# Partition sums of the later modulation vectors: 32 columns of ones in four column groups, then one product that turns rows into columns

## The chip, the cores and the metric

One core of one Trainium2 chip. The time is the device time of one execution in microseconds (us), and a kernel is given by the median of its runs. PE is TensorE (matrix products), DVE is VectorE, ACT is ScalarE, POOL is GpSimd, and SP issues the DMAs. SBUF is the memory on the core that the engines read, with 128 partitions; PSUM is the memory that PE writes its products into.

## The reference, cut to what matters

The block is one layer of a hybrid backbone: a combined input projection feeds four GLA heads and four mLSTM heads, an output projection follows, and then a SwiGLU MLP with a 3x3 depthwise convolution. Each sub-layer is modulated by vectors computed from the condition `c`:

```python
c_act = jax.nn.silu(c)
mod = (c_act @ w_mod + b_mod)[:, None, :]
sh1, sc1, gt1, sh2, sc2, gt2 = jnp.split(mod, 6, axis=-1)
...
x = x + gt1 * merge_groups(...)
h2 = rmsnorm(x, g_norm2) * (1 + sc2) + sh2
x = x + gt2 * conv_ffn(h2, ...)
```

`c` is one vector of 2048 numbers, `w_mod` is 2048 x 12288, all in float32. The model width is 2048, there are 512 latent tokens and 256 context tokens, and the MLP is 5504 wide. The change is in how `gt1`, `sh2`, `sc2` and `gt2` are summed, which the kernel calls regions 2, 3, 4 and 5.

## The kernel before, in words

Every large product is made of three products of rounded halves (`mm3`: high x high, high x low, low x high), so each 512 KB block of weights is loaded, cast to a high half on ACT (L89) and to the remaining low half on DVE (L90), and then used by 24 or 36 products on PE. `load_split` does this. The loaded block lives in the pool `wraw`, which has four buffers; the high and low halves have two buffers each. The projections of the eight heads come first (`project_steps`, eight blocks for each head, tiles `a`), with the recurrent stages of the head before woven into them by `weave`; then the gates (`unit`, tiles `ga`), the output projection (`wo`), and the MLP, where `up_gate` and `up_val` alternate (tiles `ug` and `uv`, eight blocks of weights each, the number behind them is the group of four feature tiles) and `down_block` follows (`dn`). While the products of `uv` run, DVE makes the convolution of the group before, tile `cv`, with eight instructions for each of four tiles.

The modulation vectors of regions 2 to 5 are made beside all this. Each region has four groups of 512 outputs. For each group, `mod_chunk` loads eight 512 KB blocks of `w_mod` into the same four `wraw` buffers. In each block the even half is multiplied by its part of `c_act` and summed on DVE (L252, L255, tile `sum0`), the odd half is scaled on ACT (L253, L256) and summed on POOL (L257, tile `sum1`). After the eighth, POOL adds the two sums (L259). What is left is a tile of 128 partitions x 512 columns whose sum over the partitions is wanted, as four columns of 128. `mod_end` makes it with four PE products, each with 128 x 128 of the tile as the stationary operand and one column of ones as the moving one, and DVE adds the bias.

These steps are "fillers": a list of small functions that `load_split` works off, so many for each block of weights:

```python
credit[0] += rate[0]
while credit[0] >= 1:
    credit[0] -= 1
    if fillers:
        fillers.pop(0)()
```

`rate` is 2 for blocks 3 to 7 of an mLSTM head (and 0 for blocks 0 to 2), and 1.5 in the gates, the output projection and the MLP, so there one block of weights takes one filler and the next two. `mod_fillers` lists the eight chunks of a group, `lag - 1` empty fillers, and `mod_end`. With `lag` 3 a group takes 11 fillers in regions 2 to 4. In region 5 it takes 10, behind 20 empty ones.

The products of heads and fillers are kept in program order on PE (`pinned` and `keep_in_program_order`); the order of the other engines is made by a scheduler, which also decides which buffer of a pool a tile gets. Small PSUM results, among them `mc` of `mod_end`, `pg` and `po` of the mLSTM heads, and the new `mr`, share the pool `psB`, which has two buffers.

Of the kernel before, what the change touches and what calls it, by code (L numbers as in the profile page):

```python
# [11 lines left out]
F32 = mybir.dt.float32  # L12
# [6 lines left out]
P = 128  # L19
# [25 lines left out]
C_ONE = C_SA + 32  # L45
# [24 lines left out]
def block_kernel(ctx: ExitStack, tc: tile.TileContext, a: dict, out: bass.AP):  # L70
    nc = tc.nc
    V, S, G, PE = nc.vector, nc.scalar, nc.gpsimd, nc.tensor

    def pool(stack, name, bufs=1, space=None, waits="pool"):
        if space is None:
            return stack.enter_context(tc.tile_pool(name=name, bufs=bufs, reuse_waits=waits))
        return stack.enter_context(tc.tile_pool(name=name, bufs=bufs, space=space))
# [7 lines left out]
    def add(o, x, y):  # L85
        V.tensor_tensor(out=o, in0=x, in1=y, op=ALU.add)
# [23 lines left out]
    keep = pool(ctx, "keep")  # L110
    cst = keep.tile([P, C_END], F32, name="cst")
# [12 lines left out]
    def cc(off, n=P, p=P):  # L124
        return cst[0:p, off : off + n]

    ident = cc(C_ID)
    ones = cst[:, C_ONE : C_ONE + 1].to_broadcast([P, P])
# [6 lines left out]
    def psb(name, shape=(P, T)):  # L135
        return psB.tile(list(shape), F32, name=name, tag="psb")
# [20 lines left out]
    fillers = []  # L157
# [84 lines left out]
    def mod_chunk(region, n, kp, parts):  # L242

        name = f"m{region}_{n}_{kp}"
        raw = wraw.tile([P, 2, T], F32, name=f"raw_{name}", tag="raw")
        nc.sync.dma_start(raw, a["w_mod2"][region - 2, n, kp])
        if kp == 0:
            parts += [sum_tile(i, name) for i in range(2)]
        dv, po = parts
        ce, co = (csil[:, 2 * kp + i : 2 * kp + i + 1] for i in range(2))  # L250
        if kp == 0:
            V.tensor_scalar(out=dv, in0=raw[:, 0, :], scalar1=ce, scalar2=None, op0=ALU.mult)  # L252
            S.activation(po, raw[:, 1, :], AF.Copy, scale=co)  # L253
        else:
            V.scalar_tensor_tensor(out=dv, in0=raw[:, 0, :], scalar=ce, in1=dv, op0=ALU.mult, op1=ALU.add)  # L255
            S.activation(raw[:, 1, :], raw[:, 1, :], AF.Copy, scale=co)  # L256
            G.tensor_tensor(out=po, in0=po, in1=raw[:, 1, :], op=ALU.add)  # L257
        if kp == KP - 1:
            G.tensor_tensor(out=po, in0=po, in1=dv, op=ALU.add)  # L259

    def mod_end(region, n, parts):

        po = parts[1]
        ps = psb(f"mc{region}_{n}", (P, 4))
        for i in range(4):
            tc.keep_in_program_order(PE.matmul(ps[:, i : i + 1], po[:, P * i : P * i + P], cst[:, C_ONE : C_ONE + 1],
                                               start=True, stop=True))
        o = modc[region][:, 4 * n : 4 * n + 4]
        add(o, ps, bmod[:, 16 * region + 4 * n : 16 * region + 4 * n + 4])
        if region == 4:  # L270
            V.scalar_tensor_tensor(out=o, in0=o, scalar=1.0, in1=gn2[:, 4 * n : 4 * n + 4], op0=ALU.add, op1=ALU.mult)

    def mod_fillers(regions, lag):

        for region in regions:
            for n in range(4):
                parts = []
                for kp in range(KP):
                    fillers.append(lambda r=region, n=n, kp=kp, p=parts: mod_chunk(r, n, kp, p))
                fillers.extend([lambda: None] * (lag - 1))  # L280
                fillers.append(lambda r=region, n=n, p=parts: mod_end(r, n, p))

    def sum_tile(i, name):
# [218 lines left out]
    for c0, n, hs, m in ((0, T, hx, gm[0]), (T, TC, hc, gm[1])):  # L502
        ps = psb(f"gm{c0}", (P, n))
        for k in range(KT):
            g = 32 * (k % 4)
            parts = [h[k].bitcast(F32) for h in hs]
            if hs is hx and not 4 <= k < 8:
                parts = [xl[k]]
            for i, part in enumerate(parts):
                mm(ps[g : g + 32, :], wsm[:, k, :], part, start=(k < 4 and i == 0),  # L510
                   stop=(k >= 12 and i == len(parts) - 1), skip_group_check=True)
# [360 lines left out]

    yT = []
    mod_fillers((2, 3, 4), 3)
    pinned[0] = True
    preps = [{} for _ in range(H)]
# [142 lines left out]
        return fp.tile([P, T], F32, name=f"sum{i}_{name}", tag=f"g{'hl'[i]}10")  # L1019

    rate[0] = 1.5
    fillers += [lambda: None] * 20
    mod_fillers((5,), 2)

    def up_gate(q):
        accs = unit(a["w_up4"][2 * q] if q < 10 else a["w_up3"][0], f"ug{q}", *h2, n=QUADS[q])
# [152 lines left out]
def build(nc, arrays):  # L1179
    ins = {k: nc.dram_tensor(f"in_{k}", v.shape, mybir.dt.from_np(v.dtype), kind="ExternalInput").ap()  # L1180
           for k, v in arrays.items()}
    out = nc.dram_tensor("out_0", (KT, P, T), F32, kind="ExternalOutput").ap()
    with tile.TileContext(nc) as tc:
        block_kernel(tc, ins, out)
# [8 lines left out]
```

## Time and profile before

| what | value |
|---|---|
| median of three runs | 2600.23 us (2597.21 to 2606.91) |
| the profiled execution, its own time | 2597.59 us |
| span of that profile | 2595.9 us |
| busy share of PE, DVE, ACT, POOL | 98%, 52%, 34%, 9% |
| granted clock of TensorE, mean | 0.994 |

The span is the time from the first to the last instruction in the profile; 1.7 us of the execution lie around it. A row of the timeline gives the start in us from the start of the span, the length, the engine, the line, the operation, and the tiles (output, an arrow, inputs), with the shape of the weights as partitions*columns and of the moving operand. A number with an arrow in brackets is the idle time of the engine before the row and what ended it. Products on PE overlap, so their rhythm is read from start to start, not from their lengths. Float32 products appear as two rows each, so the 64 products of `mod_end` are 128 rows. `PEld` is the loading of weights.

### The profile page before, as it was taken

How to read it: one execution, taken by the hardware profiler on the slowest of the kernel's cores; microseconds unless marked ns; L12 is line 12 of the kernel's file. 1: busy time of each engine (PE TensorE's matmuls, PEld its weight loads, DVE VectorE, ACT ScalarE, POOL GpSimd, SP SyncE). 2: the span in 40 equal slices, each digit the busy share in tenths (PEclk: the TensorE clock that was granted, in tenths of full speed). 3: DMA queues.
4: the chain of work that ended last, by engine and by line, in shares of the span. 5: the costliest groups of instructions: out<-in, count | busy, mean ns of one | idle time of the engine just before them, and what ended most of it. 6: DMA issues, size and time to landing. Idle time of an engine off the chain costs nothing.

```text
span 2595.9 us, 31962 instructions
## 1 busy us (share of the span) xinstructions
PE 2541.1 (98%) x12882; PEld 2134.8 (82%) x12882; DVE 1356.0 (52%) x1969; ACT 873.9 (34%) x1289; POOL 228.1 (9%) x183
## 2 busy tenths in 40 slices
PE   6999999999999999999999999999999999999998
PEld 4887888888897888878878888888888888888887
DVE  6557765543334465458576336532653365336544
ACT  4225543332333343334433123312331233123332
POOL 0000001021222323210321000000000000000001
PEclk9999999999999999989999999999999999999999
DMA  9741112121333666532654222322232223222333
GB/s 383 269 155 34 33 41 90 66 98 66 122 122 126 214 226 216 199 114 101 211 178 141 96 97 97 98 97 98 98 98 98 97 98 97 96 96 87 100 97 102
DMA packets 96349, 321.39 MB, mean 124 GB/s; under 512 B 10884, under 2 KB 15304, under 8 KB 96200
## 3 DMA queue, kind: packets, MB, share of 16 engines
q1 hardware_dynamic: 96200, 319.34, 35.8%
q8 instruction: 101, 1.65, 0.3%
q14 instruction: 48, 0.39, 0.0%
HBM read 315.10 MB, written 4.19 MB: 123 GB/s over the span
## 4 chain that ended last, share of the span: by engine, by line
PE 89%; DVE 4%; DMA 4%; issue 1%; ACT 1%; POOL 1%; SPq 0%; POOLq 0%; ACTq 0%; DVEq 0%
PE a L95 18%; PE ug L95 18%; PE dn L95 17%; PE uv L95 17%; PE wo L95 6%; PE ga L95 5%; PE po L95 3%; DMA raw_m<-in_w_mod 2%; PE sl L95 1%; PE ps_m L95 1%; DVE cv L1040 1%; PE dl L95 1%; PE cst L95 0%; POOL sum_m L257 0%; PE s L95 0%
## 5 line engine op out<-in xcount | busy, mean ns | idle before, releaser
L95 PE MATMUL ug<-h2h,hi_ug 128*128 128x512 f32 x688 | 269.0, 392 | 1.6 <-ACT h2h L999 1.6
L95 PE MATMUL uv<-h2h,hi_uv 128*128 128x512 f32 x688 | 268.6, 390 | 1.5 <-ACT hi_uv L89 1.5
L95 PE MATMUL uv<-h2h,lo_uv 128*128 128x512 f32 x688 | 268.5, 390 | 1.4 <-DVE lo_uv L90 1.4
L95 PE MATMUL ug<-h2l,hi_ug 128*128 128x512 f32 x688 | 268.4, 390 | 0.0
L95 PE MATMUL ug<-h2h,lo_ug 128*128 128x512 f32 x688 | 268.4, 390 | 0.0
L95 PE MATMUL uv<-h2l,hi_uv 128*128 128x512 f32 x688 | 268.4, 390 | 0.0
L95 PE MATMUL dn<-gh,hi_d 128*128 128x512 f32 x644 | 250.5, 389 | 0.0
L95 PE MATMUL dn<-gl,hi_d 128*128 128x512 f32 x644 | 250.5, 389 | 0.0
L95 PE MATMUL dn<-gh,lo_d 128*128 128x512 f32 x644 | 250.5, 389 | 0.0
L1040 DVE SCALAR_TENSOR_TENSOR cv<-pad,cwt,cv 128x512 f32<-128x512 f32 x344 | 242.8, 765 | 10.6 <-ACT cv L1038 9.1
L90 DVE TENSOR_TENSOR lo_ug<-raw_ug,hi_ug 128x1024 fp32r<-128x1024 f32 (+1 forms) x88 | 107.3, 1220 | 240.0 <-ACT hi_ug L89 240.0
L257 POOL TENSOR_TENSOR sum_m<-sum_m,raw_m 128x512 f32<-128x512 f32 x112 | 175.6, 1568 | 576.2 <-ACT raw_m L256 335.7
L90 DVE TENSOR_TENSOR lo_uv<-raw_uv,hi_uv 128x1024 fp32r<-128x1024 f32 (+1 forms) x88 | 105.6, 1200 | 181.1 <-ACT hi_uv L89 180.6
L90 DVE TENSOR_TENSOR lo_d<-raw_d,hi_d 128x1024 fp32r<-128x1024 f32 x82 | 98.8, 1205 | 165.5 <-ACT hi_d L89 164.6
L89 ACT CAST hi_ug<-raw_ug 128x1024 fp32r<-128x1024 f32 (+1 forms) x88 | 90.9, 1033 | 266.6 <-PE ug L95 199.2
L89 ACT CAST hi_d<-raw_d 128x1024 fp32r<-128x1024 f32 x82 | 85.1, 1037 | 278.7 <-PE dn L95 224.4
L255 DVE SCALAR_TENSOR_TENSOR sum_m<-raw_m,csil,sum_m 128x512 f32<-128x512 f32 x112 | 97.9, 874 | 150.6 <-DMA raw_m<-in_w_mod 150.4
L89 ACT CAST hi_uv<-raw_uv 128x1024 fp32r<-128x1024 f32 (+1 forms) x88 | 90.9, 1033 | 251.0 <-PE uv L95 180.9
L95 PEld LDWEIGHTS uv<-h2h,lo_uv 128*128 128x128 f32 x688 | 129.6, 188 | 29.6 <-DVE lo_uv L90 2.7
L95 PEld LDWEIGHTS ug<-h2h,hi_ug 128*128 128x128 f32 x688 | 129.9, 189 | 28.9 <-ACT h2h L999 1.9
L95 PEld LDWEIGHTS uv<-h2h,hi_uv 128*128 128x128 f32 x688 | 129.4, 188 | 28.9 <-ACT hi_uv L89 2.0
L95 PEld LDWEIGHTS ug<-h2l,hi_ug 128*128 128x128 f32 x688 | 129.7, 189 | 27.0
(304 smaller groups left out, 5220.4 us busy)
## 6 DMA issues: line engine op xcount, KB each, us to landing
raw_m<-in_w_mod SPq DMA_DIRECT2D x192, 512.0 KB, 4.4
raw_ug<-in_w_up SPq DMA_DIRECT2D x80, 512.0 KB, 3.2
raw_uv<-in_w_up SPq DMA_DIRECT2D x80, 512.0 KB, 3.2
raw_d<-in_w_down SPq DMA_DIRECT2D x79, 512.0 KB, 3.3
raw_h<-in_w_heads SPq DMA_DIRECT2D x64, 512.0 KB, 3.2
raw_ga<-in_w_gates SPq DMA_DIRECT2D x32, 512.0 KB, 3.4
raw_wo<-in_w_out SPq DMA_DIRECT2D x32, 512.0 KB, 4.3
xl<-in_xT SPq DMA_DIRECT2D x16, 256.0 KB, 4.8
```

The costliest lines, as they stand in the source:

```text
L89: S.copy(hi, x)
L90: return V.tensor_tensor(out=lo, in0=x, in1=hi.bitcast(F32), op=ALU.subtract).ins
L95: ins = PE.matmul(*args, **kw)
L255: V.scalar_tensor_tensor(out=dv, in0=raw[:, 0, :], scalar=ce, in1=dv, op0=ALU.mult, op1=ALU.add)
L257: G.tensor_tensor(out=po, in0=po, in1=raw[:, 1, :], op=ALU.add)
L1040: V.scalar_tensor_tensor(out=t3, in0=src, scalar=w, in1=t3, op0=ALU.mult, op1=ALU.add)
```

## The change

`mod_end` is split. The new `mod_sums` makes four products with the roles exchanged: 32 columns of ones are the stationary operand, 128 columns of the sum tile the moving one, and the results go to the partitions 0 to 31, 32 to 63, 64 to 95 and 96 to 127 of one PSUM tile `mr`. Each of them is a row of 128 sums, repeated 32 times. ACT copies the 128 x 128 tile to SBUF (`mrow`, one buffer). `mod_end` then makes one product with `mrow` as the stationary operand and columns 0, 32, 64 and 96 of the identity as the moving one, which yields the four columns. The DVE addition stays.

In `mod_fillers` the last empty filler becomes `mod_sums`, so `mod_sums` stands one filler ahead of `mod_end`. Regions 2 to 4 keep 11 fillers for a group. Region 5 goes from 20 empty fillers and 10 for each group to 16 empty ones and 11 for each group; both make 60.

```diff
+    def mod_sums(region, n, parts):
+
+        po = parts[1]
+        ps = psb(f"mr{region}_{n}", (P, P))
+        for i in range(4):
+            tc.keep_in_program_order(PE.matmul(ps[32 * i : 32 * i + 32, :], ones[:, 0:32], po[:, P * i : P * i + P],
+                                               start=True, stop=True, skip_group_check=True))
+        parts.append(keep.tile([P, P], F32, name=f"mrow{region}_{n}", tag="mrow"))
+        with tc.high_priority():
+            S.copy(parts[2], ps)
+
     def mod_end(region, n, parts):
 
-        po = parts[1]
         ps = psb(f"mc{region}_{n}", (P, 4))
-        for i in range(4):
-            tc.keep_in_program_order(PE.matmul(ps[:, i : i + 1], po[:, P * i : P * i + P], cst[:, C_ONE : C_ONE + 1],
-                                               start=True, stop=True))
+        tc.keep_in_program_order(PE.matmul(ps, parts[2], ident[:, 0 : P : 32], start=True, stop=True))
         o = modc[region][:, 4 * n : 4 * n + 4]
         add(o, ps, bmod[:, 16 * region + 4 * n : 16 * region + 4 * n + 4])
...
-                fillers.extend([lambda: None] * (lag - 1))
+                fillers.extend([lambda: None] * (lag - 2))
+                fillers.append(lambda r=region, n=n, p=parts: mod_sums(r, n, p))
                 fillers.append(lambda r=region, n=n, p=parts: mod_end(r, n, p))
...
-    fillers += [lambda: None] * 20
-    mod_fillers((5,), 2)
+    fillers += [lambda: None] * 16
+    mod_fillers((5,), 3)
```

Where `mod_sums` and `mod_end` fall relative to each other depends on the fillers that one block of weights takes. In ten of the sixteen groups they belong to different blocks, with 24 or more rows of PE between them. In five, all at rate 1.5 (groups 0 and 3 of region 3, group 2 of region 4, groups 0 and 3 of region 5), they belong to one block and four products stand between them. In one, group 1 of region 2, nothing stands between them.

Three places show it. The first is PE in the last mLSTM head (head 7), where `pg70` and `pg71` are the two products that feed the exponentials of that head through `psB`. Before:

```order
L95 MATMUL pg70_6622<-negg_95,cst_58 128x512
L95 MATMUL pg71_6635<-negg_95,cst_58 128x512
L95 MATMUL ga0_0_6576<-hTh2_554,hi_ga0_1_6649 128x512
L95 MATMUL ga0_0_6576<-hTl2_555,hi_ga0_1_6649 128x512
L95 MATMUL ga0_0_6576<-hTh2_554,lo_ga0_1_6650 128x512
```

and now:

```order
L95 MATMUL pg70_6634<-negg_95,cst_58 128x512
L95 MATMUL pg71_6647<-negg_95,cst_58 128x512
L266 MATMUL mr2_3_6666<-sum1_m2_3_0_6331,cst_58 32x128 x4
L95 MATMUL ga0_0_6588<-hTh2_554,hi_ga0_1_6661 128x512
L95 MATMUL ga0_0_6588<-hTl2_555,hi_ga0_1_6661 128x512
L95 MATMUL ga0_0_6588<-hTh2_554,lo_ga0_1_6662 128x512
```

The sums of group 3 of region 2 (`mr2_3`) now stand directly behind the two products that fill both buffers of `psB`; the old `mc2_3` stood 24 rows further on, behind the products `cst70` and `cst71`, where it still stands in its new form.

The second place is group 1 of region 2, on PE and on ACT, at the end of block 2 of head 6 (tiles `a6`). Now, on PE:

```order
L95 MATMUL a6_5_5255<-lo_h6_2_5423,hch5_748 128x384
L95 MATMUL a6_5_5255<-hi_h6_2_5422,hcl5_749 128x384
L266 MATMUL mr2_1_5564<-sum1_m2_1_0_4905,cst_58 32x128 x4
L275 MATMUL mc2_1_5571<-cst_58,mrow2_1_5569 128x4
L95 MATMUL a6_0_5250<-hTh6_939,hi_h6_3_5559 128x512
```

and on ACT, where `mrow2_1` is the copy that the second of these products needs:

```order
L146 ACTIVATE scr5_5611<-var5_5610 128x4
L147 ACTIVATE rs5_5612<-scr5_5611 128x4
L89 CAST hi_h6_4_5651<-raw_h6_4_5650 128x1024
L270 COPY mrow2_1_5569<-mr2_1_5564 128x128
L253 ACTIVATE sum1_m2_2_0_5659<-raw_m2_2_0_5656,csil_61 128x512
```

Before, one row `mc2_1` of four products stood in the place of the two on PE, and the sum of the next group followed the cast on ACT directly; the copy has moved in between, behind the cast.

The third place is SP, which issues the loads, in `up_val` of group 1 (`raw_uv1`, blocks of weights) with the chunks of group 2 of region 5 (`raw_m5_2`). Before:

```order
L164 DMA raw_uv1_3_10512<-in_w_up4 128x1024
L246 DMA raw_m5_2_0_10518<-in_w_mod2 128x1024
L246 DMA raw_m5_2_1_10524<-in_w_mod2 128x1024
L164 DMA raw_uv1_4_10553<-in_w_up4 128x1024
L246 DMA raw_m5_2_2_10559<-in_w_mod2 128x1024
L164 DMA raw_uv1_5_10588<-in_w_up4 128x1024
L246 DMA raw_m5_2_3_10594<-in_w_mod2 128x1024
L246 DMA raw_m5_2_4_10599<-in_w_mod2 128x1024
L164 DMA raw_uv1_6_10628<-in_w_up4 128x1024
```

and now:

```order
L164 DMA raw_uv1_3_10579<-in_w_up4 128x1024
L246 DMA raw_m5_2_2_10585<-in_w_mod2 128x1024
L246 DMA raw_m5_2_3_10590<-in_w_mod2 128x1024
L164 DMA raw_uv1_4_10619<-in_w_up4 128x1024
L246 DMA raw_m5_2_4_10625<-in_w_mod2 128x1024
L164 DMA raw_uv1_5_10654<-in_w_up4 128x1024
L246 DMA raw_m5_2_5_10660<-in_w_mod2 128x1024
L246 DMA raw_m5_2_6_10665<-in_w_mod2 128x1024
L164 DMA raw_uv1_6_10694<-in_w_up4 128x1024
```

The loads of region 5 stand two chunks earlier relative to the blocks of `uv1`. Over the whole of region 5, the units `uv0`, `ug1`, `uv1` and `ug2` carried 4, 10, 10 and 8 chunks by the count of fillers, and now carry 8 each.

## The prediction

> **What bounds the kernel now.** I read the head of the page and its chain of waits first, then the groups of PE with the shapes kept apart.
>
> ```profile
> span 2595.9 us, 31962 instructions
> PE 2541.1 (98%) x12882; PEld 2134.8 (82%) x12882; DVE 1356.0 (52%) x1969; ACT 873.9 (34%) x1289; POOL 228.1 (9%) x183
> PE 89%; DVE 4%; DMA 4%; issue 1%; ACT 1%; POOL 1%; SPq 0%; POOLq 0%; ACTq 0%; DVEq 0%
> L266 PE MATMUL mc<-cst,sum_m 128*128 128x1 f32 x128 | 15.1, 239 | 0.0
> ```
>
> PE is busy for 98% of the span and 89% of the chain lies on it. So what the change saves on PE it saves in full, and what it makes PE wait it loses in full. The stage touched, `mc`, is 128 rows with 15.1 us of busy time: even if it vanished the kernel would gain 0.6%. The change can only be small unless it makes PE wait. About 0.5% (13 us) is what a measurement of this kernel can tell from no change.
>
> **The old products.** Lengths overlap, so the price is read from start to start, in the timeline of PE around one group (the starts of three products, the eight rows of `mc`, three products):
>
> ```profile
> 839.53 0.39 PE L95 MATMUL ga<-hTl,hi_ga 128*128 128x512 f32 x1
> 839.76 0.39 PE L95 MATMUL ga<-hTh,lo_ga 128*128 128x512 f32 x1
> 839.99 0.95 PE L266 MATMUL mc<-cst,sum_m 128*128 128x1 f32 x8
> 840.80 0.49 PE L95 MATMUL ga<-hTh,hi_ga 128*128 128x512 f32 x1
> 841.12 0.40 PE L95 MATMUL ga<-hTl,hi_ga 128*128 128x512 f32 x1
> 841.36 0.40 PE L95 MATMUL ga<-hTh,lo_ga 128*128 128x512 f32 x1
> ```
>
> The eight rows take 840.80 - 839.99 = 0.81 us, and the next product 0.32 instead of 0.23: 0.90 us for a group, 14.4 us for sixteen.
>
> **The new products (term 1).** The kernel already has products with 32 columns in four column groups, in the early modulation, and products of a copied tile with a few columns:
>
> ```profile
> 152.24 0.28 PE L95 MATMUL a<-lo_h,hTh 128*128 128x256 f32 x1
> 152.36 0.28 PE L95 MATMUL a<-hi_h,hTl 128*128 128x256 f32 x1
> 152.57 1.93 PE L95 MATMUL ps_m<-raw_m,cact 128*32 128x256 f32 x32
> 154.43 0.39 PE L95 MATMUL a<-hi_h,hTh 128*128 128x256 f32 x1
> 154.66 0.28 PE L95 MATMUL a<-lo_h,hTh 128*128 128x256 f32 x1
> 155.97 0.50 PE L95 MATMUL ps_m<-cst,rows_m 128*128 128x2 f32 x4
> 156.33 0.42 PE L95 MATMUL a<-hi_h,hch 128*128 128x384 f32 x1
> ```
>
> There 32 rows of 256 columns take 1.86 us. `mr` has 8 rows of 128 columns: 0.23 us if the columns count (an eighth), 0.47 if the rows count (a quarter). Entering costs 0.09 (0.21 against 0.12 from start to start), leaving 0.11 (0.23 against 0.12). So `mr` costs 0.43 to 0.67; I take 0.55. The new `mc` is two rows of the kind of which four take 0.36: 0.18, and 0.09 for the product behind it as above, 0.27. Together 0.82 against 0.90: sixteen groups save 1.3 us. The bounds: 3.2 us saved at 0.43, and 5.9 us lost if the four groups didn't overlap at all, with 0.10 for each of eight rows as in the old `mc` (0.80 + 0.20 + 0.27 = 1.27).
>
> **The copy and who stands behind it (term 2).** Sixteen copies of 128x128 on ACT cost 0.28 us each by the nearest row (`kn`), 4.5 us on an engine that is busy for 34%; they are hidden unless PE needs the copy at once. It does in group 1 of region 2.
>
> ```profile
> 23.78 0.37 ACT L224 COPY rows_m<-ps_m 128x256 f32<-128x256 f32 x1 [0.94 <-PE ps_m L95]
> 24.20 0.61 PE L95 MATMUL ps_m<-cst,rows_m 128*128 128x2 f32 x4 [0.50 <-ACT rows_m L224]
> 518.80 0.28 ACT L549 ACTIVATE kn<-a 128x128 f32<-128x128 f32 x1 [0.46 <-PE a L95]
> 643.87 0.95 PE L266 MATMUL mc<-cst,sum_m 128*128 128x1 f32 x8
> 644.68 0.48 PE L95 MATMUL a<-hTh,hi_h 128*128 128x512 f32 x1
> 644.20 0.20 ACT L147 ACTIVATE rs<-scr 128x4 f32<-128x4 f32 x1
> 644.31 1.03 ACT L89 CAST hi_h<-raw_h 128x1024 fp32r<-128x1024 f32 x1
> 839.96 1.05 ACT L89 CAST hi_ga<-raw_ga 128x1024 fp32r<-128x1024 f32 x1 [3.90 <-PE ga L95]
> ```
>
> The sums are done at 643.87 + 0.55 = 644.4, but the copy stands behind the cast on ACT, which ends at 645.34. The copy ends at 645.62, PE has it 0.05 later (23.78 + 0.37 to 24.20), and `mc` takes 0.18: the next product starts at 645.85 instead of 644.68. That is 1.2 us lost; 0.6 if the copy came before the cast. In the five groups with four products in between, the cast runs to 841.01 and the copy to 841.3, while PE gets there at 839.99 + 0.55 + 0.92 = 841.46. The cover is 0.15 us thin: I take 0.3 us for all five, between 0 and 1.5.
>
> **The two buffers of `psB` (term 3).** `mr2_3` is placed right behind `pg70` and `pg71`, which hold both buffers. It must wait until ACT has read `pg70`: `qs` and four exponentials `ed`.
>
> ```profile
> 772.13 1.13 PE L95 MATMUL pg<-negg,cst 4*128 4x512 f32 x4
> 773.19 0.50 PE L95 MATMUL ga<-hTh,hi_ga 128*128 128x512 f32 x1
> 774.16 1.76 ACT L825 ACTIVATE ed<-pg,acol 128x512 f32<-128x512 f32 x4
> 775.80 0.71 ACT L815 ACTIVATE qs<-pg,gccol 128x512 f32<-128x512 f32 x1
> 793.94 0.70 PE L95 MATMUL po<-c,qs 128*128 128x258 f32 x2 [1.14 <-DVE ed L83]
> 799.76 0.67 PE L95 MATMUL po<-c,qs 128*128 128x258 f32 x2 [0.69 <-DVE dn L859]
> 805.10 0.67 PE L95 MATMUL po<-c,qs 128*128 128x258 f32 x2 [0.24 <-DVE ob L866]
> 810.90 0.67 PE L95 MATMUL po<-c,qs 128*128 128x258 f32 x2 [0.70 <-DVE ob L866]
> ```
>
> PE reached this place at 773.19; the exponentials end at 775.92. All `ga` products queue behind the waiting one: 2.7 us. What is late next may be nothing: PE then waits for DVE four times in this head, 2.8 us in all, and a PE that comes 2.7 us later finds some of that done. I let half of it, 1.4, come back. A stop also has a second price, the clock, seen in `uv1`:
>
> ```profile
> 1330.15 0.39 PE L95 MATMUL uv<-h2h,lo_uv 128*128 128x512 f32 x1
> 1332.09 0.50 PE L95 MATMUL uv<-h2h,hi_uv 128*128 128x512 f32 x1 [1.54 <-ACT hi_uv L89]
> 1332.00:1337.50 5.50, 4.89 (x13) 3.63 (x14) 4.72 (x4) 2.53 (x4) 2.76 (x2) 0.69 0.85 247
> PE uv L95 <- DVE lo_uv L90: 1.4, 3, 0.6
> ```
>
> After that wait of 1.54 us the granted clock was 0.69 over 5.5 us (the third number from the end of the row by stretches, the third of these), a loss of 0.31 x 5.5 = 1.7 us. The last row, of PE's waits, is used below. I take half of it for the new stop, 0.9. Term 3: 2.7 - 1.4 + 0.9 = 2.2, between -0.1 (all comes back) and 4.4 (nothing does, clock lost). The Trainium skill (TensorE: Matmul & The Clock Gate, Part 1) says that the clock halves only after a window of about 3.4 us without work; by that rule the 0.9 falls away and the sum below would be 2.0. The stop in `uv1`, shorter than that, speaks against it.
>
> **The loads of region 5 (term 4).** The row on `lo_uv` and the 1.54 for `hi_uv` are PE's waits in `uv1` (1294 to 1345): 2.9 us, and 1.7 of clock, 4.6 in all. From 1170 to 1390 PE waits for no other block of weights. There the convolution on DVE delays the chunks, the chunks hold `wraw` buffers, and the weights come late. The change takes two of ten chunks out of `uv1` and `ug1` and puts four more into `uv0`, which has no wait now. But in `uv1` more loads of chunks stand ahead of `raw_uv1_5`. I take a loss of 0.5 us, between a gain of 4.6 (the waits are cured) and a loss of 6 (they stay as they are, and `uv0` gets the like, with a little more).
>
> **What costs nothing.** `mod_sums` comes one block of weights earlier, 24 products or 5.4 us, so PE could meet POOL's last addition.
>
> ```profile
> 1036.40 2.15 POOL L259 TENSOR_TENSOR sum_m<-sum_m,sum_m 128x512 f32<-128x512 f32 x1
> 1049.52 0.72 PE L266 MATMUL mc<-cst,sum_m 128*128 128x1 f32 x6
> ```
>
> This is the tightest of regions 2 to 4: the addition ends at 1038.55, PE would be there at 1044.1. That leaves 5.5 us. Region 5 keeps two fillers between its last chunk and the sums. Without the cover, each group would pay what is missing.
>
> **The sum.** -1.3 + 1.2 + 0.3 + 2.2 + 0.5 = +2.9 us. The profiled span of 2595.9 becomes 2598.8; its execution (2597.59, 1.7 us around the span) 2600.5. The median of the runs stands 2.6 above that execution, at 2600.23, so I predict 2603.1 us. The lower bounds add up to -3.2 + 0.6 + 0 - 0.1 - 4.6 = -7.3, the upper to 5.9 + 1.2 + 1.5 + 4.4 + 6 = +19.
>
> **The rivals.**
> First, the new spacing of region 5 cures `uv1` and the stop at `mr2_3` comes back in full: -1.3 + 1.2 + 0.3 - 0.1 - 4.6 = -4.5 us, 2595.7. For it speaks that `uv1` loses a fifth of its chunks; against it, the order of SP there.
> Second, the column groups don't overlap for so short products: +5.9 in place of -1.3, 2610.3. For it speaks only that no row here has 128 columns on 32; against it, the 1.86 us for 32 rows, which is 0.06 for each where one lasts 0.38.
> Third, slower than can be overlooked: weights starve in `uv0`, `ug1` and `ug2` as they do in `uv1`, since eight chunks now compete with the blocks of each unit for the four `wraw` buffers. It decides once blocks arrive a microsecond behind PE in each of them. `uv1` has paid its 4.6 already; the three others would pay the same: 3 x 4.6 = 13.8 in place of the 0.5 of term 4, so 2603.1 - 0.5 + 13.8 = 2616.4. For it speaks that `uv0` doubles its chunks beside the convolution; against it, that `ug1` carries ten now without a wait.
> That the change doesn't do what it says: if leaving the column groups cost as much as the products save, term 1 is 0 and the time 2604.4, which no measurement tells from the forecast.
>
> **How the numbers follow.** The forecast 0.62 (2598 to 2608), the first rival 0.18, the second 0.10, the third 0.10. Slower by over 0.5% means above 2613: nearly all of the third and a little of the second, 0.10. Faster by over 0.5% means below 2587, which no case gives; 0.04 for what I don't see. The rest, 0.86, is no change. The range takes in the first two rivals and the spread of the runs: 2593 to 2613.
>
> **What would show it.** Right: `mr` rows 0.4 to 0.7 us from start to start, new `mc` under 0.3; a wait of PE for ACT of about 2.7 us near 773 and one of a microsecond near 645; the waits for `po` behind it shorter; the sum of waits in `uv0` to `ug2` within some microseconds of 2.9. Wrong: `mr` over 1 us, waits of `mr` for POOL, waits for `hi_uv` or `lo_uv` in several units, a low granted clock at several places.

## The result, and the profile after

| | median of the runs | runs | ratio to the kernel before | 95% interval |
|---|---|---|---|---|
| kernel before | 2599.72 us | 16 | | |
| changed kernel | 2610.50 us | 16 | 1.0037 | 1.0030 to 1.0044 |
| changed kernel, once more in a later set (before there: 2598.59) | 2609.62 us | 5 | 1.0042 | 1.0030 to 1.0054 |

The change makes the kernel 0.4% slower: 10.8 us between the medians, 9.6 by the ratio, which is not the quotient of the medians. The forecast was 2603.1 us with a range to 2613 and "no change" at the bound of 0.5%. Both hold, the middle is 7 us off, and the reason is a step that the forecast costed at nothing. That the range reaches far enough is luck: its upper end was drawn for other losses. The bound itself was too coarse, for the interval here is 0.07% to either side. One run of x3_old23 below took 11399 us for a reason that nothing here shows; it stays out of its ratio. The profiled execution of the changed kernel took 2607.17 us, 9.58 more than that of the kernel before.

The head of its page and four of PE's waits (us in total, times, longest):

```profile
span 2605.4 us, 32045 instructions
PE 2540.1 (97%) x12914; PEld 2123.6 (82%) x12914; DVE 1361.3 (52%) x1969; ACT 875.2 (34%) x1305; POOL 230.2 (9%) x183
...
PE po L95 <- DVE ed L83: 4.2, 1, 4.2
PE uv L95 <- ACT hi_uv L89: 4.0, 2, 3.4
PE mr L266 <- POOL ed L837: 2.8, 1, 2.8
...
PE mc L275 <- ACT mrow L270: 1.2, 1, 1.2
```

PE works as long as before (2540.1 against 2541.1 us) in a span that is 9.5 us longer: the loss is waiting. Two of the four waits were forecast by name and size, `mr` in head 7 and `mc` behind its copy. (The third row names POOL, but the readers of `pg70` that `mr` had to wait for are on ACT: the last of the four exponentials `ed` ends there at 783.10, 0.15 us before the product.) One of 4.2 us was not forecast at all: `po` for `ed`. Two longer waits, `ss_l` (19.0 us, before 18.6) and `sl` (7.3, before 4.5), lie ahead of 500 us, where the change has not begun; PE is 0.33 us behind there.

The large products are the same and stand in the same order in both kernels, so the start of one and the same product in both traces gives a ledger. Behind is the start after less the start before:

| product (start before) | behind | since the row above | what lies between |
|---|---|---|---|
| 500.06 | +0.33 | +0.33 | the start of the span |
| 509.69 | +0.78 | +0.45 | `mr2_0`, moved here |
| 546.54 | +6.90 | **+6.12** | **the mLSTM stage of head 4** |
| 562.38 | +6.22 | -0.68 | the old `mc2_0` gone, the new one there |
| 644.68 | +7.34 | +1.12 | group 1 of region 2: `mc` behind the copy |
| 735.59 | +7.19 | -0.15 | group 2 of region 2 |
| 776.72 | +12.02 | +4.83 | `mr2_3` and what follows it |
| 816.20 | +9.16 | -2.86 | the rest of head 7 |
| 1137.60 | +8.25 | -0.91 | regions 3 and 4 |
| 1166.45 | +6.76 | -1.49 | output norm, no step of the change lies here |
| 1390.03 | +9.07 | +2.31 | region 5 |
| 2585.78, the last | +9.44 | +0.37 | the rest |

The row on the output norm, where nothing was changed, shows how far two executions can differ in one stretch: 1.5 us.

**Head 4.** The timelines of DVE (128x1024 rows are the low halves of weights) and, in the second block, of PE there:

```profile
539.74 0.75 DVE L255 SCALAR_TENSOR_TENSOR sum_m<-raw_m,csil,sum_m 128x512 f32<-128x512 f32 x1 [2.30 <-DMA raw_m<-in_w_mod]
...
545.20 0.75 DVE L255 SCALAR_TENSOR_TENSOR sum_m<-raw_m,csil,sum_m 128x512 f32<-128x512 f32 x1 [3.12 <-DMA raw_m<-in_w_mod]
545.87 0.28 DVE L83 TENSOR_TENSOR ed<-ed,s 128x128 f32<-128x128 f32 x1
546.07 2.29 DVE L90 TENSOR_TENSOR lo_h<-raw_h,hi_h 128x1024 fp32r<-128x1024 f32 x1
548.28 0.68 DVE L83 TENSOR_TENSOR ed<-ed,s 128x512 f32<-128x512 f32 x1
```

```profile
549.01 1.05 PE L95 MATMUL po<-c,qs 128*128 128x258 f32 x2 [4.21 <-DVE ed L83]
549.85 3.29 PE L95 MATMUL po<-v,ed 128*128 128x258 f32 x8
552.79 0.58 PE L95 MATMUL a<-hTh,hi_h 128*128 128x512 f32 x1
```

DVE takes its instructions in order. It stands idle 2.30 and 3.12 us in front of a chunk's sum whose load has not come, with the last `ed` of the head behind it, and PE waits 4.21 us for that `ed`. PE's last product `s`, which the row at 545.87 reads, was done at 542.54 (it starts at 541.52 and takes 1.02), so it is not `s` that held `ed` back. The same place in the kernel before, DVE and then PE:

```profile
541.70 0.29 DVE L83 TENSOR_TENSOR ed<-ed,s 128x128 f32<-128x128 f32 x1 [1.01 <-PE s L95]
541.93 1.23 DVE L90 TENSOR_TENSOR lo_h<-raw_h,hi_h 128x1024 fp32r<-128x1024 f32 x1
543.07 0.68 DVE L83 TENSOR_TENSOR ed<-ed,s 128x512 f32<-128x512 f32 x1
...
543.80 0.70 PE L95 MATMUL po<-c,qs 128*128 128x258 f32 x2
544.34 1.91 PE L95 MATMUL po<-v,ed 128*128 128x258 f32 x8
```

There the last chunk's sum stands ahead of the first `ed` (at 535.16), none stands between the `ed`, and `po` has no stop. Group 1's loads of `w_mod` start at 514.21, 531.95 and 543.18 in the kernel before, and at 514.54, 523.10, 528.74, 535.48 and 541.87 in the changed one. So the two sums with the idle time are those of its chunks 3 and 4, which have moved between the `ed`, with 1 and 2 ahead of them. The tile `sum1` has one buffer. In the kernel before, group 1 could not have it until `mc2_0` had read group 0's, at 561.6 us. Now `mr2_0` reads it at 510.1, 51 us earlier, and the scheduler fills the opening with group 1's chunks. POOL and SP show why each comes late, for chunk 4:

```profile
540.55 1.29 POOL L257 TENSOR_TENSOR sum_m<-sum_m,raw_m 128x512 f32<-128x512 f32 x1 [5.10 <-ACT raw_m L256]
541.87 0.33 SPq L246 DMA_DIRECT2D raw_m<-in_w_mod  x1
```

Its load can start only when the sum of the chunk before it on POOL has given the buffer back, at 541.84, and its own sum on DVE waits for that load until 545.20. `ed` and PE wait behind it.

**The half clock behind a stop.** The stretches behind three of the new stops (in head 7, in head 4, and in `uv1` behind the wait of 3.4 us for `hi_uv`), in the view by windows (us, then busy time and instructions of five engines, the granted clock third from the end, DMA share, GB/s):

```profile
784.64:787.94 3.30, 3.30 (x10) 2.55 (x8) 0.00 (x0) 1.65 (x3) 2.16 (x4) 0.52 0.20 53
549.85:552.79 2.94, 2.94 (x10) 2.36 (x8) 0.00 (x0) 0.19 (x1) 0.00 (x0) 0.52 0.64 202
1337.80:1340.80 3.00, 3.00 (x8) 2.30 (x7) 2.96 (x2) 1.75 (x2) 2.01 (x2) 0.50 0.89 318
```

Each is some 3 us at half the clock and costs about 1.5 us on top of the stop.

**The products.** PE around one group of region 3:

```profile
887.82 0.39 PE L95 MATMUL ga<-hTh,lo_ga 128*128 128x512 f32 x1
888.13 0.43 PE L266 MATMUL mr<-sum_m,cst 128*32 128x128 f32 x8
...
888.83 0.39 PE L95 MATMUL ga<-hTl,hi_ga 128*128 128x512 f32 x1
...
893.84 0.39 PE L95 MATMUL ga<-hTh,lo_ga 128*128 128x512 f32 x1
894.07 0.28 PE L275 MATMUL mc<-cst,mrow 128*128 128x4 f32 x2
...
894.52 0.40 PE L95 MATMUL ga<-hTl,hi_ga 128*128 128x512 f32 x1
```

From 887.82 to 888.83 are 1.01 us, less two rhythms of 0.227: `mr` costs 0.56. From 893.84 to 894.52 are 0.68, less the same: `mc` costs 0.23. Together 0.79 against 0.90 for the old form. The other groups of regions 3 to 5 give the same.

**Group 1 of region 2 and head 7** on PE:

```profile
650.19 0.42 PE L266 MATMUL mr<-sum_m,cst 128*32 128x128 f32 x8
651.78 0.39 PE L275 MATMUL mc<-cst,mrow 128*128 128x4 f32 x2 [1.16 <-ACT mrow L270]
652.02 0.48 PE L95 MATMUL a<-hTh,hi_h 128*128 128x512 f32 x1
...
783.25 0.43 PE L266 MATMUL mr<-sum_m,cst 128*32 128x128 f32 x8 [2.81 <-POOL ed L837]
783.60 0.50 PE L95 MATMUL ga<-hTh,hi_ga 128*128 128x512 f32 x1
```

Both stops are there as forecast: 1.16 us behind the copy, 2.81 us for the two buffers of `psB`.

### The profile page after: what moved, and what is told of

Read it like the earlier page. It is cut to its first block, busy times and chain, and to the rows that moved or that the text cites. A ratio compares the mean times of both kernels' runs of the same rounds, so it can differ in the third digit from the quotient of the medians.

```text
span 2605.4 us, 32045 instructions
## 1 busy us (share of the span) xinstructions
PE 2540.1 (97%) x12914; PEld 2123.6 (82%) x12914; DVE 1361.3 (52%) x1969; ACT 875.2 (34%) x1305; POOL 230.2 (9%) x183
## 4 chain that ended last, share of the span: by engine, by line
PE 88%; DVE 6%; DMA 2%; issue 2%; ACT 1%; POOL 1%; SPq 0%; POOLq 0%; DVEq 0%; ACTq 0%
PE ug L95 17%; PE dn L95 17%; PE a L95 17%; PE uv L95 16%; PE wo L95 7%; PE ga L95 5%; PE po L95 3%; DMA raw_m<-in_w_mod 2%; DVE cv L1049 2%; PE ps_m L95 1%; PE sl L95 1%; PE dl L95 1%; DVE lo_uv L90 1%; DVE ex L80 0%; DVE sq_l L86 0%
## 5 line engine op out<-in xcount | busy, mean ns | idle before, releaser
L95 PEld LDWEIGHTS ug<-h2h,lo_ug 128*128 128x128 f32 x688 | 129.7, 189 | 27.8 <-DVE lo_ug L90 0.9
```

Of the source, the lines that this page charges most:

```text
L95: ins = PE.matmul(*args, **kw)
```

## The experiments

The theory after the reading: 6 us are lost in head 4, because the earlier read of group 0 gives the sum tile back early. About 2 us are lost at `mr2_3`, about 1 at group 1 and 1 to 2 in region 5, and the products themselves save a little. The rival: the new form costs (column groups, copies), wherever it stands. A label stands for one kernel; all ratios are to the kernel before in the same set of runs.

| kernel | median, us | before beside it | ratio | 95% interval |
|---|---|---|---|---|
| x1_old20 | 2605.82 | 2598.83 | 1.0025 | 1.0013 to 1.0037 |
| x2_own_sum | 2607.27 | 2598.83 | 1.0028 | 1.0018 to 1.0039 |
| x3_old23 | 2609.02 | 2598.83 | 1.0033 | 1.0022 to 1.0045 |
| x4_old5 | 2608.84 | 2598.83 | 1.0037 | 1.0023 to 1.0050 |
| x10_place | 2598.39 | 2599.54 | 0.9999 | 0.9988 to 1.0010 |
| x6_space5 | 2602.52 | 2599.54 | 1.0010 | 0.9999 to 1.0021 |
| x8_dist5 | 2616.65 | 2599.54 | 1.0065 | 1.0050 to 1.0080 |
| x9_place_dist | 2616.12 | 2599.54 | 1.0058 | 1.0043 to 1.0073 |
| x12_dist5b | 2598.88 | 2598.82 | 1.0004 | 0.9995 to 1.0013 |
| x11_place_dist | 2597.40 | 2598.82 | 0.9998 | 0.9989 to 1.0007 |
| x13_late20 | 2603.40 | 2598.59 | 1.0017 | 1.0007 to 1.0027 |
| a_again (the changed kernel) | 2609.62 | 2598.59 | 1.0042 | 1.0030 to 1.0054 |

**x1_old20: group 0 of region 2 in the old form.** `mod_end_old` is the old `mod_end`.

```diff
+                if (region, n) == (2, 0):
+                    fillers.append(lambda: None)
+                    fillers.append(lambda r=region, n=n, p=parts: mod_end_old(r, n, p))
+                    continue
```

> The changed kernel with group 0 of region 2 summed in the old way and at its old place (four products by one column of ones, right behind the load of its result). Theory (early release: the sums of this group, now done some 50 us earlier, free the sum tile, so that group 1's chunks move on DVE and ACT into head 4's mLSTM stage, ahead of ed, and PE stops there for about 4.4 us and then runs 1.9 us longer at half clock): the stop of po for ed near 548 us shrinks from 4.2 to about 1 us and the time falls by about 6 us against the changed kernel, to about 2604. Rival (the time was lost at the new products themselves, at ACT's copy or in region 5): within 1 us of the changed kernel, about 2610, and the stop near 548 us stays.

The stop of `po` for `ed` in head 4 is gone from the list of waits altogether. The time came out at 2605.82, 4.7 below the changed kernel by the medians and 3 by the ratios, between the theory (6) and the rival (1), and its runs spread from 2601 to 2613. The profiled one of them lost 5.7 us elsewhere, for no reason that its trace shows (last section), so the size stayed open. x13_late20 was made for it.

**x2_own_sum: the early release alone, without any new product.** In the kernel before:

```diff
-        return accp.tile([P, T], F32, name=f"sum{i}_{name}", tag=f"sum{i}")
+        return accp.tile([P, T], F32, name=f"sum{i}_{name}", tag="sumx" if i == 1 and name.startswith("m2_1_") else f"sum{i}")
```

> The kernel before, with nothing new on PE or ACT: only group 1 of region 2 gets a buffer of its own for its sum tile, so that its chunks need not wait until group 0 has been summed. Theory (early release alone is what costs in head 4): about 6 us slower than the kernel before, about 2606, with a stop of po for ed of about 4 us in head 4. Rival (the new products, the copy or the second buffer of psB are needed for that stop): within 1 us of the kernel before, and the stop stays near 1 us.

The kernel has no `mr`, no copy and nothing new in `psB`, and it is 8.4 us slower than the one beside it (7.3 by the ratio). DVE (first three rows) and PE in its head 4, then DVE in its head 5:

```profile
546.69 0.75 DVE L255 SCALAR_TENSOR_TENSOR sum_m<-raw_m,csil,sum_m 128x512 f32<-128x512 f32 x1 [3.17 <-DMA raw_m<-in_w_mod]
547.36 0.28 DVE L83 TENSOR_TENSOR ed<-ed,s 128x128 f32<-128x128 f32 x1
...
549.77 0.68 DVE L83 TENSOR_TENSOR ed<-ed,s 128x512 f32<-128x512 f32 x1
...
550.50 1.23 PE L95 MATMUL po<-c,qs 128*128 128x258 f32 x2 [3.91 <-DVE ed L83]
...
633.56 0.75 DVE L255 SCALAR_TENSOR_TENSOR sum_m<-raw_m,csil,sum_m 128x512 f32<-128x512 f32 x1 [2.42 <-DMA raw_m<-in_w_mod]
634.23 0.88 DVE L83 TENSOR_TENSOR ed<-ed,s 128x128 f32<-128x128 f32 x2
```

The same idle time of DVE, the same stop. So the release alone makes it, and the rival falls. Of the 2.4 us above the 6 expected, 1.8 have a place too. With a buffer of its own for group 1, the common one is also free early for group 2, whose chunks move ahead of `ed` in head 5 (the last two rows), where PE falls behind by another 1.8 us. That the edit would do this was overlooked in the expectation.

**x13_late20 and a_again: the place of one group, new form kept.**

```diff
+                    if (region, n, kp) == (2, 1, 1):
+                        fillers.append(lambda r=region, n=n, kp=kp, p=parts, q=first: (mod_chunk(r, n, kp, p), mod_end(2, 0, q)))
+                        continue
...
+                if (region, n) == (2, 0):
+                    first = parts
+                    fillers.extend([lambda: None] * (lag - 1))
+                    fillers.append(lambda r=region, n=n, p=parts: mod_sums(r, n, p))
+                    continue
```

> The changed kernel with one group's sums put later: mr2_0 stands where the old mc2_0 stood, its mc one block behind. All chunks keep their slots, all sixteen groups keep the new products, region 5 and mr2_3 stay as in the change. Theory (early release of the sum tile costs about 6 us in head 4): 4 to 6 us faster than the changed kernel that runs beside it, about 2604.5, no wait of po for ed of over 1.2 us in head 4. Rival (the place of this group is worth nothing): within 1.5 us of the changed kernel.

> The changed kernel once more, on the same chip and in the same rounds as the run with the late sums, as its mate: about 2610.5, ratio 1.0037.

2603.40 against 2609.62 on the same chip, with intervals that do not meet: 6.2 us, or 0.25% between the two ratios, for moving the four products of one group one filler later. Head 4 in its trace, DVE and then PE:

```profile
541.26 0.29 DVE L83 TENSOR_TENSOR ed<-ed,s 128x128 f32<-128x128 f32 x1 [1.02 <-PE s L95]
541.49 1.23 DVE L90 TENSOR_TENSOR lo_h<-raw_h,hi_h 128x1024 fp32r<-128x1024 f32 x1
542.63 0.68 DVE L83 TENSOR_TENSOR ed<-ed,s 128x512 f32<-128x512 f32 x1
...
543.36 0.70 PE L95 MATMUL po<-c,qs 128*128 128x258 f32 x2
543.90 1.91 PE L95 MATMUL po<-v,ed 128*128 128x258 f32 x8
545.45 0.58 PE L95 MATMUL a<-hTh,hi_h 128*128 128x512 f32 x1
```

DVE waits for PE's `s` and not for a load, `po` has no stop, and the eight rows of `po` take 1.55 us from start to start where they took 2.94 at half clock. Nothing else in this kernel differs from the change but `mc2_0`, which had to move along, so the 6 us belong to this place. The ledgers of all traces say the same: between the products that start at 500.06 and 562.38 before, the five with the early release fall 5.4 to 6.0 us behind (the changed kernel twice, x2_own_sum, x3_old23, x4_old5), and the three without it lie between -0.4 and 0.0 (x1_old20, x10_place, x13_late20).

**x3_old23: group 3 of region 2 in the old form**, with `(region, n) == (2, 3)` in the edit of x1_old20.

> The changed kernel with group 3 of region 2 in the old way and place. In head 7 the changed kernel stops for 2.8 us in mr2_3, runs 3.3 us at half clock behind it, and has about 5 us more behind the kernel before there; of this most is regained in four waits of po for DVE. Theory (comes back as term 3 had it, net 2.2 predicted, 1.6 read from the traces): 1 to 2.5 us faster than the changed kernel, about 2609. Rival (nothing comes back): 4.4 us faster, about 2606. Second rival (all comes back): same within 0.5 us.

2609.02 is 1.5 below the changed kernel, and intervals of 0.1% do not tell this from nothing. The ledgers do: between the products that start at 735.59 and 815.52 before, this trace falls 0.2 us behind, and the five with `mr2_3` at its new place 2.0, 3.5, 2.1, 2.8 and 3.4 (the changed kernel twice, x13_late20, x1_old20, x4_old5). The stop and its half clock cost 1.8 to 3.3 us net, 2.5 in the mean, and half of the gross loss of 4.4 comes back in the waits of `po`. "Nothing comes back" and "all comes back" both fall: PE's waits for `po` in this head are 2.8 us before and 0.6 to 1.6 in the five. The one trace of x3_old23 is thin ground for the size, though. In x12_dist5b, where this stretch is that of the kernel before, PE falls 2.7 us behind at a wait of 1.91 us for `ob` and the half clock that follows it; x2_own_sum does the like (2.08 us).

**x4_old5 and x6_space5: region 5.** x4 is the changed kernel with region 5 in the old form and spacing, x6 the kernel before with only the new spacing. The edit of x6 against the kernel before:

```diff
-    fillers += [lambda: None] * 20
-    mod_fillers((5,), 2)
+    fillers += [lambda: None] * 16
+    mod_fillers((5,), 3)
```

> The changed kernel with region 5 as before: old products, the old 20 empty fillers and ten fillers for each group. Theory (the new spacing gathers the waits of uv1 in one stop of 3.4 us and adds a wait in uv0; term 4 predicted 0.5, the traces read 1.6 to 2): 1.5 to 2 us faster than the changed kernel, about 2608.5. Rival (the difference of the two traces there is that of two executions): same within 0.5 us.

> The kernel before with one part of the change alone: region 5 starts after 16 instead of 20 empty fillers and has eleven instead of ten for each group; the products are the old ones at their old place behind the last chunk. Theory (the first four chunks more in uv0 give a wait there, uv1's waits stay; term 4): 0.5 to 2 us slower than the kernel before, about 2600.5. Rival 1 (uv1 is cured): 4.6 us faster, about 2594.5. Rival 2 (starvation in several units): 10 us slower or more.

x4 has the same ratio as the changed kernel (1.0037), x6 stands 3 us above the kernel before, with an interval from -0.3 to 5.5. From the starts of the same products (1166.45 to 1390.03), region 5 loses 0.2 to 2.3 us, 1.3 in the mean, in the five traces that have it as in the change, and gains 0.0 and 0.3 in the two of x2_own_sum and x4_old5 that have it as before; but in the trace of x6 it gains 0.6. Part of that is the clock: behind the stop of 3.15 us in x6's `uv1`, which ends at 1329.51, the granted clock stays at 1.00, while a half-clock stretch follows the like stop in the other five. The new spacing costs something between nothing and 3 us, which these runs cannot settle; the cure (2594.5) and the starvation (10 us or more) are both excluded. PE's waits in x6 show what it does:

```profile
PE uv L95 <- ACT hi_uv L89: 3.6, 2, 3.1
PE uv L95 <- DVE lo_uv L90: 0.5, 1, 0.5
```

The waits that lay scattered over `uv1` (1.54 for `hi_uv`, 1.4 for `lo_uv`) are gathered in one of 3.1 us, with a smaller one in `uv0`; their sum goes from 2.9 to 4.1 us.

**x10_place: all the new products, at other places.** Sums where the old products stood, `mc` with the second chunk of the next group, and region 5 at its old pace, behind 19 empty fillers:

```diff
+                    if kp == 1:
+                        ends, due = due, []
+                        fillers.append(lambda r=region, n=n, kp=kp, p=parts, e=ends: (mod_chunk(r, n, kp, p), *(f() for f in e)))
+                        continue
...
-                fillers.extend([lambda: None] * (lag - 2))
+                last = (region, n) == (regions[-1], 3)
+                fillers.extend([lambda: None] * (1 if last else lag - 1))
                 fillers.append(lambda r=region, n=n, p=parts: mod_sums(r, n, p))
-                fillers.append(lambda r=region, n=n, p=parts: mod_end(r, n, p))
+                due.append(lambda r=region, n=n, p=parts: mod_end(r, n, p))
+        fillers.extend(due)
...
-    fillers += [lambda: None] * 16
-    mod_fillers((5,), 3)
+    fillers += [lambda: None] * 19
+    mod_fillers((5,), 2)
```

> The changed kernel with its new products for all sixteen groups, but at other places: the sums mr stand where the old products stood (one block of weights later than in the change), and mc is put a block or more behind them, so that the copy is always done. All chunks of regions 2 to 4 keep their old slots; region 5 keeps its old pace and starts one filler earlier. Theory (the loss of the change is one of place: early release, mc2_1 behind its copy, mr2_3 behind pg; the products themselves save about 0.1 us for each group): 1 to 2 us faster than the kernel before, about 2598, and no stop of more than 2 us for ed in head 4 or for mr in head 7. Rival (the form itself costs: entering and leaving the column groups, the copies on ACT): 3 us or more slower than the kernel before, about 2603 or above.

2598.39 against 2599.54, a ratio of 0.9999 up to 1.0010. All sixteen groups have the new products and copies, and the loss is gone. The rival, which put 2603 or more here, falls. This run takes all four losses of place away at once, the spacing of region 5 among them, and prices none of them singly. Its waits between 530 and 830 us, all of them:

```profile
PE po L95 <- DVE ob L882: 1.2, 1, 1.2
PE po L95 <- DVE ed L83: 1.0, 1, 1.0
PE po L95 <- DVE dn L875: 0.4, 1, 0.4
```

No `mr`, no `mc`, and `ed` with the 1.0 us that the kernel before had as well (1.1). The saving on PE, 16 x 0.11 = 1.8 us, is too small to be told from nothing by these runs.

**x8_dist5, x9_place_dist, x12_dist5b, x11_place_dist: can `uv1` be cured?** The waits of `uv1`, put down to chunks beside the convolution, were the one gain in sight for either kernel. x8 puts the chunks of region 5 on other fillers in the kernel before; x9 does so on top of x10_place.

```diff
-    fillers += [lambda: None] * 20
     mod_fillers((5,), 2)
+    fillers[26:26] = [lambda: None] * 10
+    fillers[12:12] = [lambda: None] * 10
```

> The kernel before with the chunks of region 5 put on other slots: 10, 2, 10, 2, 8 of the 32 in ug0, uv0, ug1, uv1 and ug2, so that few lie beside the convolution on DVE. Theory (the waits of uv1 come from chunks that stand behind the convolution on DVE and hold the buffers of the raw blocks): the waits for hi_uv and lo_uv in uv1 (2.9 us) and the half clock behind them (1.7) go, 4 to 4.6 us faster than the kernel before, about 2595. Rival (the blocks of uv1 are late for another reason): within 1 us of the kernel before, and the waits stay. Second rival (ten chunks in ug0 bring a wait of their own): 1 us or more slower.

> Both together: the new products at the places of the run with other places, and the chunks of region 5 on 10, 3, 10, 1 and 8 slots. Theory: the two gains add up to 5 to 6 us against the kernel before, about 2594. Rival: one of the two is not there, 2595 to 2599.

A miss, 17 us the wrong way in both, in one wait. For x8 the second rival had named the place, not the size; for x9 nothing had. ACT (first two rows) and PE of x8_dist5 in `ug0`:

```profile
1189.24 0.72 ACT L253 ACTIVATE sum_m<-raw_m,csil 128x512 f32<-128x512 f32 x1 [1.70 <-DVE h2l L80]
1194.51 1.04 ACT L89 CAST hi_ug<-raw_ug 128x1024 fp32r<-128x1024 f32 x1 [4.55 <-DMA raw_ug<-in_w_up]
...
1195.61 0.79 PE L95 MATMUL ug<-h2h,hi_ug 128*128 128x512 f32 x1 [18.11 <-ACT hi_ug L89]
```

The first chunk's sum could not start before `h2l` was done. Until then the chunks kept the buffers that the blocks of `ug0` needed. The waits of `uv1` were gone, as the theory had it. So the chunks were moved once more, in x12 for the kernel before and in x11 on top of x10_place (there `mc` of region 5 goes with the third chunk):

```diff
+    f, m, skip = list(fillers), [], lambda: None
+    for g in range(4):
+        c = f[10 * g : 10 * g + 8]
+        if g:
+            c[0] = lambda e=f[10 * g - 1], c0=c[0]: (e(), c0())
+        m += c + [skip]
+    m += f[39:]
+    fillers[:] = [skip] * 8 + m[:4] + [skip] * 8 + m[4:20] + [skip] * 6 + m[20:]
```

> The kernel before with the chunks of region 5 moved again. In the first try three quarters of the loss came from chunks put at the very start of ug0: their sum tile opens only when h2 is done on DVE (near 1188 us), and until then they held buffers of the raw blocks, so that hi_ug waited 18.1 us; in uv1 the waits were gone. Now the first chunk stands behind raw_ug_5 and the 32 chunks lie 4, 4, 10, 6, 8 over ug0, uv0, ug1, uv1, ug2. Theory (the chunks beside the convolution cause uv1's waits): no long wait in ug0, uv1's waits shrink, 2 to 4.6 us faster than the kernel before, about 2596. Rival (six chunks late in uv1 are enough to keep the waits): within 1 us of the kernel before. Second rival (the sum tile is still not open): a wait for hi_ug of some microseconds in ug0, slower.

> The new products at the places of the run with other places, together with the chunks of region 5 at the slots of the run beside this one (4, 4, 10, 6, 8). Theory: the gain of those slots and the 1.3 us of the products add up, 3 to 6 us faster than the kernel before, about 2595. Rival: within 1 us of the kernel before.

PE's waits from 1170 to 1400 us in x12_dist5b:

```profile
PE uv L95 <- DVE lo_uv L90: 2.3, 2, 1.5
PE ug L95 <- DVE lo_ug L90: 1.0, 2, 0.8
```

The wait for `hi_uv` is gone, and from 1290 to 1352 us this kernel gains 4.5 us on the one before. But from 1200 to 1290, in `uv0` and `ug1`, it has lost 3.9. The rival holds in both kernels: no gain. Chunks, convolution and blocks share DVE over all five units, and in these two tries moving the chunks only moved the wait; that no order of them would gain is not shown. No kernel of this study beats the kernel before by more than the runs can tell; x11_place_dist is nearest, at 0.9998.

## Why the prediction was right in its class and 7 us off in its number

**The step that failed** is the first sentence under "What costs nothing": "`mod_sums` comes one block of weights earlier, 24 products or 5.4 us, so PE could meet POOL's last addition." It asked only what PE would meet on arriving earlier, and it was right about that: no `mr` waits for POOL's addition anywhere. It did not ask what the earlier read gives back. For group 0 of region 2 one filler earlier is not 5.4 us but 51, since between the two fillers lie block 7 of one head's projections, blocks 0 to 2 of the next (rate 0), and the mLSTM stage woven into them. In that time the one buffer of `sum1` came free, group 1's chunks moved into the stage, and an in-order DVE carried the wait for their loads to `ed` and to PE. That cost 6.1 us in the ledger, 6.2 in the runs (x13_late20 against a_again), and x2_own_sum shows that the release is enough by itself. No term, bound or rival held it: the third rival has slow loads in front of an engine, but in region 5. With it the forecast would have been 2603.1 + 6.2 = 2609.3, against 2609.6 and 2610.5 measured; that it comes so near owes something to errors of the other terms that cancel.

The other steps, in order:

- **Term 1, the products, -1.3 us.** Right. `mr` costs 0.56 (0.55 forecast) and `mc` 0.23 (0.27), so sixteen groups save 1.8. The column groups overlap, and the second rival (1.27 for a group) falls with x10_place.
- **Term 2, the copy, +1.2 for group 1 and 0.3 for five groups.** Right for group 1: 1.16 of wait, 1.12 in the ledger. The five groups pay nothing. The copy of the first ends at 850.33 (it starts at 850.07 and takes 0.26), the `mc` behind it starts at 850.63, so the cover is 0.3 us where 0.15 was forecast. (The lower bound of 0.6 for group 1 does not follow from the rows beside it: a copy that starts at 644.42 and takes 0.28, 0.05 and 0.18 us for what follows give 644.93, a loss of 0.25. The sum of the lower bounds would be -7.6 instead of -7.3.)
- **Term 3, `mr2_3`, +2.2.** Right in the sum, by luck: two of its parts are off by 0.7 and 0.8 us, and they cancel. The stop is 2.81 (2.7 forecast). The half clock costs 1.6 where 0.9 was taken. And of the 2.86 us that head 7 gives back, 0.65 is the new `mc` in place of the old, so 2.2 comes back where 1.4 was let. 2.81 + 1.6 - 2.2 = 2.2 in this trace, 1.8 to 3.3 over five against x3_old23.
- **Term 4, region 5, +0.5.** Not refuted and not settled: 1.3 in the mean of five traces, -0.6 in that of the spacing alone, -0.3 to 5.5 us in the runs of x6_space5. The first rival (a cure) and the third (starvation in three units) fall. `uv0` loses 1.6 us near 1240, as the term said, and `uv1` keeps its waits.
- **That PE's waits decide** and its busy time does not: right, by the first two rows of the profile after.

## What to carry to other kernels

When a read is moved earlier, ask two questions: what must it wait for, and what does it set free. A tile with one buffer is also a brake on the work that uses it next, and a scheduler that finds it open can put that work in front of something else on an engine that works in order, as it did here on DVE. Measure the step in the place where it lands (here rate 0 made one filler worth 51 us), not by its usual length. A wait that a busy stage shows cannot be priced as a gain before it is known where it will go: the waits of `uv1` were gone or smaller in four kernels, two of them 17 us slower and none faster by more than the runs can tell.

## What was not expected of the hardware

The forecast took half of a loss of 1.7 us for the clock, because the stop was short. In the changed kernel's trace the stops of 2.81, 3.38 and 4.21 us, and in that of x2_own_sum one of 2.08 (head 7), were each followed by a stretch of 3.4 us at a granted clock of 0.50, starting 0.2 to 1.5 us after PE had resumed. All five traces with the stop in head 4 and all five with the one of 2.81 have the like. The stop of 1.16 us at 651.78 was not followed by one: the products behind it start 0.23 us apart.

The length of a stop does not decide it. The wait of `cdec` near 212 us is 1.13 us in every trace (one of 0.6 lies just ahead of it), and a half-clock stretch sets in near its end in eight of the fourteen kept traces (the clock is 0.52 from 213 to 220 us in a_again, 1.00 from 208 to 218 in the changed kernel's first trace). The wait of `sl` that ends between 454 and 459 us is 3.1 us in thirteen, and a stretch lies there in seven (0.64 from 456.2 to 461 us in x6_space5, 1.00 from 455.2 to 460 in the changed kernel). So the price of a stop holds for a trace, not for a kernel. The Trainium skill (TensorE: Matmul & The Clock Gate, Part 1) gives an idle window of about 3.4 us before the clock halves; the length of the half-clock stretches agrees with such a window, the stops of 2.08 and 2.81 us that were enough do not. What decides stays open.

And the clock falls without a stop. The profiled execution of x1_old20, by windows:

```profile
485.00:495.00 10.00, 9.66 (x61) 8.07 (x60) 2.88 (x12) 2.15 (x6) 0.00 (x0) 1.00 0.01 2
495.50:509.50 14.00, 14.00 (x49) 8.89 (x49) 6.41 (x10) 3.57 (x4) 0.00 (x0) 0.53 0.11 37
510.00:520.00 10.00, 10.00 (x62) 9.45 (x61) 9.34 (x8) 1.22 (x2) 0.00 (x0) 1.00 0.16 54
```

For 14 us PE had half the clock, behind a stretch with no stop over 0.34 us, and lost 5.7 us against the same products in the kernel before. The kernels without that stretch have 1.00 there. What starts it stays open. The runs of a kernel that spread over some 10 us go with their granted clock: of the twelve of x1_old20 the two shortest (2601.1 and 2601.3 us) have a mean of 0.994, the two longest (2613.0 and 2613.1) 0.988 and 0.989. So differences of 1 to 3 us had to be read from the starts of the same products instead of from the medians, and even there a half-clock stretch more or less is 1.5 us.
